# Split first weight units, two constants DMAs, and a new order of the first products in a one-core hybrid decoder block

## Chip, core and metric

One NeuronCore of a Trainium2 chip runs the whole program in one launch. The metric is device time in microseconds (us). Engines are called by the names of the profile: PE is TensorE's matmul side and PEld its weight loads, DVE is VectorE, ACT is ScalarE, POOL is GpSimd, and SP is SyncE, which here only issues DMAs.

## What is computed

The block takes x (512 tokens by 2048 channels, float32) through one decoder layer. Cut to what matters:

```python
h = rms_norm(x, norm1_g)
proj = h @ w_in                       # 2048 x 3840: 30 tiles of 128 columns
out_a = dilated_mixture(aq, ak, av)   # 8 heads x 64
out_b = conformer_conv(bu, bg, ...)   # GLU, depthwise conv of 31 taps, LayerNorm, swish
out_c = band_attention(cq, ck, cv, 127, sinks)
x = x + concat(out_a, out_b, out_c) @ w_out
h2 = rms_norm(x, norm2_g)
x = x + (silu(h2 @ w_gate) * (h2 @ w_up)) @ w_down
```

The change touches only the start of `h @ w_in`: the four column tiles bu0, bg0, bu1, bg1 that are computed first, while x and the first weights are still on their way from HBM.

## The kernel before

Everything is held transposed: a tile of x is 128 channels by 512 tokens, so x comes in 16 tiles `xs[k]`, k = 0 to 15 (256 KB each, loaded by `load_first`). A float32 product is made of three fp32r products. A weight block is split into `wh` (its fp32r rounding, a CAST on ACT, line 242) and `wl` (the rest, a subtraction on DVE, line 229). The scaled input is split likewise by `scaled`: `hh` on ACT (line 368), `hl` on DVE (line 369). `mm3` then issues wh with hh, wh with hl and wl with hh (lines 271, 272, 273) into one PSUM bank.

The first stage, called the head here, fills four PSUM banks at once (`g4`, tile name `in`): for each k, four column tiles times three products, twelve matmuls of 128x512. All 16 values of k make 192 matmuls. Weights of the head come as units: unit 0 and unit 1 are the two 512-column halves of the first 1024-column block (k = 0 and k = 1, 256 KB each), and every later unit of the head is a whole block of 512 KB that serves two values of k. In the profile these tiles are called `w`, their halves `wh` and `wl`.

Three things set the order of the work. `pump` issues the weight DMAs on SP's queue in the order of `units`, as far as raw buffers (`RAW_PLAIN`, used in rotation) are free; calls of `load_first` lie between them on the same queue. `split_up_to` issues the CAST and the subtraction of a unit, up to two units ahead of its use; ACT and DVE work strictly down the list in which Python issued their instructions. `WARM` dummy matmuls on a tile `idle`, filled by a DVE memset, are issued on PE ahead of the head. While the head runs, ACT and DVE also square x and add the squares up (`add_square`, lines 374, 377, 378) for the RMS norm.

The per-channel constants (norm gains, convolution weights, gains and sinks) come in one array `cst` of 188 columns by one DMA, which is the first instruction on ACT's queue (line 277). Columns 0 to 15 are the gains of the first norm, used by `scaled`; the others are used after the head.

Waits are made by semaphores. The DMAs get their completion semaphores from a set of eight in turn, in the order of the DMAs. A DMA that takes over a semaphore waits in its issuing engine's instruction list until the DMA that held it before has landed.

Of the kernel before, what the change touches and what calls it, by code (L numbers as in the profile page):

```python
# [9 lines left out]
F32 = mybir.dt.float32  # L10
F32R = mybir.dt.float32r
BF16 = mybir.dt.bfloat16
# [4 lines left out]
P = 128  # L17
T = 512
NT = T // P
D = 2048  # L20
KT = D // P
HD = 64
# [5 lines left out]
N_IN = 30  # L28
# [21 lines left out]
RAW_PLAIN = "22b sb 21a 22a 11 sa 12".split()  # L50
RAW_BUFS = 8
RAW_EARLY = 5
SPLIT_BUFS = 3
X_AHEAD = 8
SPLIT_AHEAD = 2
WARM = 10

# [5 lines left out]
TH = T // 2  # L65
# [17 lines left out]
C_G1, C_G2, C_CW, C_CB, C_LG, C_LB, C_QK, C_SINK, C_ALL = 0, 16, 32, 156, 160, 164, 168, 172, 188  # L83
# [34 lines left out]
def kernel(ctx: ExitStack, tc: tile.TileContext, xT, wi, wo, wgu, wd, cst_in, outT):  # L118
    nc = tc.nc
    cp = ctx.enter_context(tc.tile_pool(name="consts", bufs=1))  # L120
# [17 lines left out]
    def slot(name, dt=F32, cols=T):  # L138
        return sp.tile([P, cols], dt, name=name, tag="s")

    def bank(name, cols=T):
        return psum["banks"].tile([P, cols], F32, name=name, tag="b")


    units = [wi[0][:, :T], wi[0][:, T:]] + [wi[u] for u in range(1, 2 * N_IN)]
    units += [wo[2 * n + half] for half in range(2) for n in OUT_ORDER[half]]


    entries, works = [], []
# [4 lines left out]
    def take(buf, key, n=1024):  # L154
        assert buf not in held
        held[buf] = key
        raws[key] = (wp.tile([P, 1024], F32, name=f"w{key}", tag=f"raw{buf}", bufs=1), n)
        return raws[key][0]

    def drop(key):  # L160
        for buf in [b for b, k in held.items() if k == key]:
            held.pop(buf)
        return raws.pop(key)

    for u, unit in enumerate(units):
        entries.append((RAW_PLAIN[u % len(RAW_PLAIN)], u, [unit]))
        works.append((u, True, nc.vector))

    def group(name, m, n, blocks):
# [41 lines left out]
    splits = {}  # L211
    at = {"entry": 0, "split": 0, "use": 0}

    def pump(limit):
        while at["entry"] < len(entries) and len(raws) < limit and entries[at["entry"]][0] not in held:
            buf, key, parts = entries[at["entry"]]
            t, o = take(buf, key, sum(p.shape[-1] for p in parts)), 0
            for part in parts:
                nc.sync.dma_start(t[:, o:o + part.shape[-1]], part)
                o += part.shape[-1]  # L220
            at["entry"] += 1
# [4 lines left out]
    def lows_now():  # L226
        while lows:
            fn, *args = lows.pop(0)
            fn(*args)  # L229
        if late_lows:  # L230
            pump(RAW_EARLY if at["use"] <= 20 else RAW_BUFS)

    def split_up_to(i):
        while at["split"] <= min(i, len(works) - 1):
            key, last, eng = works[at["split"]]
            t, n = drop(key) if last else raws[key]
            u = at["split"]
            hi = wp.tile([P, 1024], F32R, name=f"wh{u}", tag="hi", bufs=SPLIT_BUFS)
            lo = wp.tile([P, 1024], F32R, name=f"wl{u}", tag="lo", bufs=SPLIT_BUFS)
            if eng or "high" not in psum:  # L240
                eng = eng or nc.vector
                nc.scalar.copy(hi[:, :n], t[:, :n])  # L242
                lows.append((eng.tensor_sub, lo[:, :n], t[:, :n], hi[:, :n].bitcast(F32)))
                if not late_lows:
                    lows_now()
            else:
                near = psum["high"].tile([P, 1024], F32R, name=f"wn{u}", tag="h")
                nc.scalar.copy(near[:, :n], t[:, :n])
                nc.scalar.copy(hi[:, :n], t[:, :n])  # L249
                lows.append((nc.vector.tensor_sub, lo[:, :n], t[:, :n], near[:, :n].bitcast(F32)))  # L250
                if not late_lows:
                    lows_now()
            splits[u] = (hi, lo)
            at["split"] += 1
# [5 lines left out]
    def next_unit():  # L260
        sums_now()
        u = at["use"]
        at["use"] += 1
        lows_now()
        split_up_to(u + SPLIT_AHEAD)
        if not lows:
            pump(RAW_EARLY if u < 20 else RAW_BUFS)
        return splits.pop(u)

    def mm3(out, wh, wl, xh, xl, start, stop):  # L270
        nc.tensor.matmul(out, wh, xh, start=start, stop=False)  # L271
        nc.tensor.matmul(out, wh, xl, start=False, stop=False)  # L272
        nc.tensor.matmul(out, wl, xh, start=False, stop=stop)  # L273


    cst = cp.tile([P, C_ALL], F32, name="cst")
    nc.scalar.dma_start(cst, cst_in)
    xs = []

    def load_first(k):  # L280
        x = slot(f"x{k}")
        nc.sync.dma_start(x, xT[k])
        xs.append(x)

    for k in range(X_AHEAD):
        load_first(k)
        u = k if k < 2 else k // 2 + 1
        if u < RAW_EARLY and (k < 2 or k % 2 == 0):
            pump(u + 1)


    idle = slot("idle", BF16)
    nc.vector.memset(idle, 1.0)
    b = bank("idle")
    for i in range(WARM):
        nc.tensor.matmul(b, idle[:, :P], idle, start=True, stop=True)
    b = idle = None

    nhalf = cp.tile([P, 8], F32, name="nhalf")
# [4 lines left out]
    make_identity(nc, ident)  # L304
    ones = cp.tile([P, 1], F32, name="ones")
    nc.vector.memset(ones, 1.0)
    bones = cp.tile([P, 2], F32, name="bones")
    nc.vector.memset(bones, 0.0)
    nc.vector.memset(bones[0:HD, 0:1], 1.0)
    nc.vector.memset(bones[HD:P, 1:2], 1.0)  # L310

    def col(i):
        return cst[:, i:i + 1]
# [52 lines left out]
    def scaled(x, g, tag, k):  # L366
        hi, lo = slot(f"{tag}h{k}", F32R), slot(f"{tag}l{k}", F32R)
        nc.scalar.activation(hi, x, AF.Copy, scale=g)
        nc.vector.scalar_tensor_tensor(lo, x, g, hi.bitcast(F32), op0=ALU.mult, op1=ALU.subtract)
        return hi, lo  # L370

    def add_square(acc, x, k, tag):
        if k == 0:
            nc.scalar.activation(acc, x, AF.Square)
        else:
            sq = slot(f"{tag}{k}")
            nc.scalar.activation(sq, x, AF.Square)
            nc.vector.tensor_add(acc, acc, sq)
# [9 lines left out]

    g4 = [bank(f"in{j}") for j in range(HEAD4)]
    h_hl = {}  # L390
    for k in range(2):
        h_hl[k] = scaled(xs[k], col(C_G1 + k), "h", k)
        split_up_to(k)
    pump(RAW_EARLY)
    add_square(ssum, xs[0], 0, "sq")
    for k in range(KT):
        if k < 2 or k % 2 == 0:
            wh, wl = next_unit()
            o = 0
        if k + X_AHEAD < KT:  # L400
            load_first(k + X_AHEAD)
        if k + 2 < KT:
            h_hl[k + 2] = scaled(xs[k + 2], col(C_G1 + k + 2), "h", k + 2)
        if k + 1 < KT:
            add_square(ssum, xs[k + 1], k + 1, "sq")
        hi, lo = h_hl.pop(k)
        h_hi.append(hi)
        h_lo.append(lo)
        for j in range(HEAD4):
            mm3(g4[j], wh[:, o:o + P], wl[:, o:o + P], hi, lo, k == 0, k == KT - 1)  # L410
            o += P
    xs = None
    c64 = cp.tile([P, NT], F32, name="c64")
# [7 lines left out]
    def project(name):  # L421
        b = bank(name)
        for half in range(2):
            wh, wl = next_unit()
            for kk in range(8):
                k = 8 * half + kk
                s = slice(kk * P, (kk + 1) * P)
                mm3(b, wh[:, s], wl[:, s], h_hi[k], h_lo[k], k == 0, k == KT - 1)
                if kk == 3:
                    lows_now()  # L430
                if kk % 2 == 1:
                    ticks.tick()
        return b
# [348 lines left out]
    g4 = None  # L782
# [15 lines left out]
    part = {}  # L798
    for name in PROJ[HEAD4:]:
        kind, what, j = name[0], name[1], name[2:]  # L800
# [3 lines left out]
        b = project(name)  # L804
# [19 lines left out]
    b = box = boxes = shared = None  # L824
# [81 lines left out]
    for half in range(2):  # L906
        for i, n in enumerate(OUT_ORDER[half]):
            if half == 1 and i == 2:
                ticks.drain()
                b = None  # L910
                open_banks(banks=4, high=2)
            b = bank(f"o{half}_{n}")
            wh, wl = next_unit()
            for kk in range(8):
                k = 8 * half + kk
# [262 lines left out]
    for g in range(2 * NP + len(DOWN)):  # L1178
        t = g - 2 * NP
# [4 lines left out]
        else:  # L1184
            n, first, end = DOWN[t]
            blk = Down(t)
        for i, q in enumerate(ORDER):
            sums_now()
            run(evacs)
            w = next_unit()  # L1190
# [109 lines left out]
```

## Time and profile before

| What | Value |
|---|---|
| Median of 3 runs (1899.9 to 1900.35) | 1900.18 us |
| The profiled execution's own time | 1899.99 us |
| Its span, first to last instruction | 1898.2 us |
| Lies around the span | 1.79 us |
| Mean granted TensorE clock | 0.999 |
| Busy: PE, DVE, ACT, POOL | 1887.0, 1467.6, 1330.7, 996.1 us |

Times in rows of the profile are counted from the start of the span. In a timeline row the first number is the start, the second the duration, then come engine, line, operation, output and inputs; a bracket tells how long the engine was idle before and what released it. SPq and ACTq rows are the issuing of DMAs on the queues of SP and ACT, not the transfers. In rows of DMA issues the last number is the time from the start of the issue to the landing of the data.

### The profile page before, as it was taken

The numbers are of one execution on the slowest core, as the hardware profiler recorded it, in microseconds if no ns is written. First come the engines' busy times: TensorE is split into PE (matmuls) and PEld (weight loads), VectorE is DVE, ScalarE is ACT, GpSimd is POOL, SyncE is SP. The second block draws the span as 40 slices with busy tenths as digits, with TensorE's granted clock in tenths as the row PEclk, the third lists the DMA queues.
The fourth block names the chain that finished last, engine by engine and source line by source line (L and its number), as shares of the span: only waits on it lengthen the run. The fifth ranks groups of instructions, "written<-read, shape, count | busy, mean of one in ns | idle before, by whom it ended". The sixth has DMA issues, their size and how long they took to land.

```text
span 1898.2 us, 29669 instructions
## 1 busy us (share of the span) xinstructions
PE 1887.0 (99%) x10342; PEld 1636.9 (86%) x10342; DVE 1467.6 (77%) x2561; ACT 1330.7 (70%) x1855; POOL 996.1 (52%) x643
## 2 busy tenths in 40 slices
PE   9999999999999999999999999999999999999999
PEld 7888888878888888888888888888888888888888
DVE  6789978998679777777777777777787877677776
ACT  6356645453357888888888888888887777766775
POOL 0111011000002878788787878787767656565775
PEclk9999999999999999999999999999999999999999
DMA  7342242433342444445454554445456887777985
GB/s 268 88 129 79 77 130 83 112 106 117 123 140 98 141 153 162 144 149 174 141 165 139 165 168 150 155 136 187 140 167 238 269 268 263 266 249 231 315 263 202
DMA packets 136310, 320.29 MB, mean 169 GB/s; under 512 B 15584, under 2 KB 31072, under 8 KB 136160
## 3 DMA queue, kind: packets, MB, share of 16 engines
q1 hardware_dynamic: 136016, 318.31, 52.0%
q8 instruction: 81, 1.33, 0.3%
q14 instruction: 69, 0.57, 0.1%
q10 hardware_dynamic: 144, 0.10, 0.0%
HBM read 254.11 MB, written 55.84 MB: 163 GB/s over the span
## 4 chain that ended last, share of the span: by engine, by line
PE 94%; DVE 4%; ACT 1%; issue 0%; DMA 0%; SPq 0%; DVEq 0%; ACTq 0%
PE out L989 68%; PE o L271 2%; PE o L272 2%; PE o L273 2%; PE cq L271 2%; PE cq L273 2%; PE cq L272 2%; PE ak L271 1%; PE ak L273 1%; PE ak L272 1%; PE in L272 1%; PE av L271 1%; PE av L272 1%; PE in L273 1%; PE av L273 1%; PE in L271 1%
## 5 line engine op out<-in xcount | busy, mean ns | idle before, releaser
L989 PE MATMUL out<-h,wh 128*128 128x512 f32 x2464 | 588.8, 391 | 1.0 <-DVE h L899 0.8
L989 PEld LDWEIGHTS out<-h,wh 128*128 128x128 f32 x2464 | 452.7, 188 | 89.3 <-DVE h L899 1.3
L989 PEld LDWEIGHTS out<-h,wl 128*128 128x128 f32 x2464 | 316.0, 191 | 12.0
L989 PE MATMUL out<-h,wl 128*128 128x256 f32 x2464 | 319.9, 283 | 0.0
L989 PE MATMUL out<-a,wh 128*128 128x512 f32 x1232 | 296.2, 391 | 0.0
L989 PEld LDWEIGHTS out<-a,wh 128*128 128x128 f32 x1232 | 225.7, 188 | 43.6 <-ACT wh L249 0.4
L242 ACT CAST wh<-w 128x1024 fp32r<-128x1024 f32 (+1 forms) x93 | 96.8, 1041 | 113.0 <-PE o L272 48.8
L989 PEld LDWEIGHTS out<-a,wl 128*128 128x128 f32 x1232 | 159.4, 191 | 6.9
L989 PE MATMUL out<-a,wl 128*128 128x256 f32 x1232 | 161.5, 283 | 0.0
L229 DVE TENSOR_TENSOR wl<-w,wh 128x1024 fp32r<-128x1024 f32 (+1 forms) x93 | 112.3, 1209 | 45.1 <-ACT wh L242 44.7
L458 DVE SCALAR_TENSOR_TENSOR y<-bu,cst,y 128x511 f32<-128x511 f32 (+14 forms) x120 | 89.5, 746 | 0.2
L1001 DVE TENSOR_TENSOR y<-y,out 128x256 f32<-128x256 f32 x93 | 39.1, 420 | 46.1 <-PE out L989 44.4
L271 PE MATMUL cq<-hh,wh 128*128 128x512 f32 x128 | 51.2, 400 | 0.5 <-DVE mix_c L743 0.5
L271 PE MATMUL o<-mh_c,wh 128*128 128x512 f32 x128 | 51.6, 403 | 0.0
L273 PE MATMUL o<-mh_c,wl 128*128 128x512 f32 x128 | 50.5, 394 | 0.0
L272 PE MATMUL o<-ml_c,wh 128*128 128x512 f32 x128 | 50.4, 394 | 0.0
L273 PE MATMUL cq<-hh,wl 128*128 128x512 f32 x128 | 50.0, 391 | 0.0
L272 PE MATMUL cq<-hl,wh 128*128 128x512 f32 x128 | 50.0, 390 | 0.0
L1002 DVE TENSOR_TENSOR y<-y,out 128x256 f32<-128x256 f32 x101 | 42.5, 421 | 3.5
L386 POOL TENSOR_TENSOR lvr<-lvv,nhalf 128x4 f32<-128x4 f32 x1 | 1.9, 1931 | 76.7 <-DVE lvv L385 76.7
L184 POOL TENSOR_TENSOR w('s', 'g1')_5687<-w('21', 'g1')_5533,w('22', 'g1')_5531 128x1024 f32<-128x1024 f32 x1 | 2.5, 2457 | 71.0 <-DVE wl L229 71.0
L849 DVE TENSOR_TENSOR xr<-xr,o 128x512 f32<-128x512 f32 x32 | 21.8, 682 | 13.9 <-PE o L273 13.8
(3135 smaller groups left out, 4869.1 us busy)
## 6 DMA issues: line engine op xcount, KB each, us to landing
a<-od SPq DMA_DIRECT2D x175, 256.0 KB, 5.2
od<-a SPq DMA_DIRECT2D x147, 256.0 KB, 4.6
w<-in_wi SPq DMA_DIRECT2D x59, 512.0 KB, 3.6
w<-in_wo SPq DMA_DIRECT2D x32, 512.0 KB, 3.6
yd<-y SPq DMA_DIRECT2D x68, 128.0 KB, 4.8
y<-yd SPq DMA_DIRECT2D x34, 256.0 KB, 5.1
x<-in_xT SPq DMA_DIRECT2D x16, 256.0 KB, 7.5
xr<-in_xT SPq DMA_DIRECT2D x16, 256.0 KB, 3.8
```

The costliest lines, as they stand in the source:

```text
L184: eng.tensor_add(out[:, :n], raws[key[a]][0][:, :n], raws[key[b]][0][:, :n])
L229: fn(*args)
L242: nc.scalar.copy(hi[:, :n], t[:, :n])
L271: nc.tensor.matmul(out, wh, xh, start=start, stop=False)
L272: nc.tensor.matmul(out, wh, xl, start=False, stop=False)
L273: nc.tensor.matmul(out, wl, xh, start=False, stop=stop)
L386: nc.gpsimd.tensor_tensor(r, v, nhalf[:, :NT], op=ALU.pow)
L458: nc.vector.scalar_tensor_tensor(yconv[j][:, i:], hconv[j][:, :T - i], c, yconv[j][:, i:], op0=ALU.mult, op1=ALU.add)
L849: nc.vector.tensor_add(t, t, b)
L989: nc.tensor.matmul(out, lhs[:, s], rhs, start=begin, stop=x is xs[-1] and low == flip[0], skip_group_check=True)
L1001: sign(out, out if first is None else first, main)
L1002: sign(out, out, rest)
```

## The change

Unit 0 is cut into two units of 256 columns (128 KB each), so that the units are numbered one higher from there on: what was unit 1 (k = 1) is unit 2 and what was unit 2 (k = 2 and 3) is unit 3. The CAST of the new unit 0 is done on DVE. The constants come in two DMAs on ACT's queue: columns 0 to 15 as its first instruction, columns 16 to 187 after the memset of `ones`, still ahead of the first `scaled`. The twelve products of k = 0 are issued in another order, two at a time: hh with both upper halves, then hh with wl of unit 0, hl with both, hh with wl of unit 1. `scaled` of k + 2 is issued ahead of the split of the next unit. The dummy matmuls go from ten to eight, and their 512 columns are 128 columns read four times, so that the memset is of 128 columns. The tile `bones`, which nothing read, goes with its three memsets.

```diff
-WARM = 10
+WARM = 8
...
-    units = [wi[0][:, :T], wi[0][:, T:]] + [wi[u] for u in range(1, 2 * N_IN)]
+    units = [wi[0][:, :TH], wi[0][:, TH:T], wi[0][:, T:]] + [wi[u] for u in range(1, 2 * N_IN)]
...
-        entries.append((RAW_PLAIN[u % len(RAW_PLAIN)], u, [unit]))
+        entries.append((RAW_PLAIN[(u - 1) % len(RAW_PLAIN)], u, [unit]))
...
-                nc.scalar.copy(hi[:, :n], t[:, :n])
+                (nc.vector.tensor_copy if u == 0 else nc.scalar.copy)(hi[:, :n], t[:, :n])
...
-    nc.scalar.dma_start(cst, cst_in)
+    nc.scalar.dma_start(cst[:, :C_G2], cst_in[:, :C_G2])
...
     for k in range(X_AHEAD):
         load_first(k)
-        u = k if k < 2 else k // 2 + 1
-        if u < RAW_EARLY and (k < 2 or k % 2 == 0):
-            pump(u + 1)
+        if k < 2 or k % 2 == 0:
+            pump(min(k + 2 if k < 2 else k // 2 + 3, RAW_EARLY))
-    idle = slot("idle", BF16)
+    idle = slot("idle", BF16, P)
     nc.vector.memset(idle, 1.0)
     b = bank("idle")
     for i in range(WARM):
-        nc.tensor.matmul(b, idle[:, :P], idle, start=True, stop=True)
+        nc.tensor.matmul(b, idle, idle[:, None, :].to_broadcast([P, NT, P]), start=True, stop=True)
...
     nc.vector.memset(ones, 1.0)
-    bones = cp.tile([P, 2], F32, name="bones")
-    nc.vector.memset(bones, 0.0)
-    nc.vector.memset(bones[0:HD, 0:1], 1.0)
-    nc.vector.memset(bones[HD:P, 1:2], 1.0)
+    nc.scalar.dma_start(cst[:, C_G2:], cst_in[:, C_G2:])
...
-    for k in range(2):
-        h_hl[k] = scaled(xs[k], col(C_G1 + k), "h", k)
-        split_up_to(k)
+    split_up_to(0)
+    h_hl[0] = scaled(xs[0], col(C_G1), "h", 0)
+    split_up_to(1)
+    h_hl[1] = scaled(xs[1], col(C_G1 + 1), "h", 1)
+    split_up_to(2)
     pump(RAW_EARLY)
     add_square(ssum, xs[0], 0, "sq")
     for k in range(KT):
-        if k < 2 or k % 2 == 0:
+        if k + 2 < KT:
+            h_hl[k + 2] = scaled(xs[k + 2], col(C_G1 + k + 2), "h", k + 2)
+        if k == 0:
+            at["use"] = 2
+            first = [splits.pop(u) for u in range(2)]
+        elif k == 1 or k % 2 == 0:
             wh, wl = next_unit()
             o = 0
         if k + X_AHEAD < KT:
             load_first(k + X_AHEAD)
-        if k + 2 < KT:
-            h_hl[k + 2] = scaled(xs[k + 2], col(C_G1 + k + 2), "h", k + 2)
         if k + 1 < KT:
             add_square(ssum, xs[k + 1], k + 1, "sq")
         hi, lo = h_hl.pop(k)
         h_hi.append(hi)
         h_lo.append(lo)
+        if k == 0:
+            for part, u in ((0, 0), (0, 1), (2, 0), (1, 0), (1, 1), (2, 1)):
+                for j in range(2):
+                    w = first[u][part == 2][:, j * P:(j + 1) * P]
+                    nc.tensor.matmul(g4[2 * u + j], w, (hi, lo, hi)[part], start=part == 0, stop=False)
+            first = w = None
+            continue
         for j in range(HEAD4):
-            mm3(g4[j], wh[:, o:o + P], wl[:, o:o + P], hi, lo, k == 0, k == KT - 1)
+            mm3(g4[j], wh[:, o:o + P], wl[:, o:o + P], hi, lo, False, k == KT - 1)
             o += P
```

## Prediction

> **What bounds the kernel now.** I read the page first, then who PE waited for, then the first 13 us engine by engine, since all the edits lie there. From the page:
>
> ```profile
> span 1898.2 us, 29669 instructions
> PE 1887.0 (99%) x10342; PEld 1636.9 (86%) x10342; DVE 1467.6 (77%) x2561; ACT 1330.7 (70%) x1855; POOL 996.1 (52%) x643
> ```
>
> PE is idle for 11.2 us in all. Whatever delays its first products delays the end, unless a later wait shrinks. PE's waits over the whole span, by releaser (total us, times, longest):
>
> ```profile
> PE a2o L730 <- DVE a2pl L716: 2.5, 1, 2.5
> PE idle L296 <- DVE bones L308: 1.5, 1, 1.5
> PE o L271 <- DVE xr L849: 0.9, 1, 0.9
> PE out L989 <- DVE h L899: 0.8, 1, 0.8
> PE a3o L730 <- DVE a3pl L716: 0.5, 1, 0.5
> PE cq L271 <- DVE mix_c L743: 0.5, 1, 0.5
> PE in L272 <- DVE hl L369: 0.2, 1, 0.2
> PE out L989 <- ACT wh L249: 0.2, 1, 0.2
> ```
>
> After the head all releasers are DVE or ACT work that itself comes out of earlier products of PE; no DMA is among them. So these waits move along with the head and absorb nothing: a microsecond lost or won in the head should show whole at the end. The question is when the head gets going. SP's queue, and the chain that ended last within the first 13 us:
>
> ```profile
> 2.59 0.43 SPq L282 DMA_DIRECT2D x<-in_xT  x1
> 3.06 0.43 SPq L219 DMA_DIRECT2D w<-in_wi  x1
> 3.54 1.05 SPq L282 DMA_DIRECT2D x<-in_xT  x2
> 7.84 0.33 SPq L282 DMA_DIRECT2D x<-in_xT  x1
> ```
>
> ```profile
> 3.06 6.10 DMA w<-in_wi
> 9.19 1.05 ACT wh L242
> ```
>
> The rows at 2.59, 3.06 and 3.54 are x2, unit 2 (512 KB) and x3 with x4. Unit 2 lands at 3.06 + 6.10 = 9.16, and from there ACT's CAST leads on to the products of k = 2. When the two tiles of x landed (last number: us from issue):
>
> ```profile
> x<-in_xT SPq DMA_DIRECT2D x1, 256.0 KB, 5.2
> ```
>
> ```profile
> x<-in_xT SPq DMA_DIRECT2D x1, 256.0 KB, 6.3
> ```
>
> x2: 2.59 + 5.2 = 7.8; x3: 3.54 + 6.3 = 9.8. The row at 7.84 is x7, the fourteenth DMA. It takes over the semaphore that x2, the sixth, held, and it starts 0.05 us after x2 landed: a DMA whose semaphore is still held waits in its queue, and what stands behind it waits too. Now ACT, DVE and PE in the head:
>
> ```profile
> 0.73 0.41 ACTq L277 DMA_DIRECT2D cst<-in_cst  x1
> 1.17 1.28 ACT L302 ACT_TABLE_LOAD   x1 [1.17 <-PEq L1291]
> 4.07 0.72 ACT L368 ACTIVATE hh<-x,cst 128x512 fp32r<-128x512 f32 x1 [1.40 <-DMA cst<-in_cst]
> 5.07 0.62 ACT L242 CAST wh<-w 128x512 fp32r<-128x512 f32 x1 [0.28 <-DMA w<-in_wi]
> 7.73 0.63 ACT L374 ACTIVATE ssum<-x 128x512 f32<-128x512 f32 x1
> ```
>
> ```profile
> 0.91 0.48 DVE L293 MEMSET idle<- 128x512 bf16 x1 [0.91 <-PEq L1291]
> 1.61 0.06 DVE L310 MEMSET bones<- 64x1 f32 x1
> 4.82 0.75 DVE L369 SCALAR_TENSOR_TENSOR hl<-x,cst,hh 128x512 fp32r<-128x512 f32 x1 [3.16 <-ACT hh L368]
> 5.72 0.69 DVE L229 TENSOR_TENSOR wl<-w,wh 128x512 fp32r<-128x512 f32 x1
> 10.27 1.23 DVE L229 TENSOR_TENSOR wl<-w,wh 128x1024 fp32r<-128x1024 f32 x1 [1.72 <-ACT wh L242]
> ```
>
> ```profile
> 1.45 4.14 PE L296 MATMUL idle<-idle 128*128 128x512 bf16 x10 [1.45 <-DVE bones L308]
> 5.74 0.50 PE L271 MATMUL in<-hh,wh 128*128 128x512 f32 x1
> 8.89 0.39 PE L271 MATMUL in<-hh,wh 128*128 128x512 f32 x1
> 11.61 0.39 PE L271 MATMUL in<-hh,wh 128*128 128x512 f32 x1
> 12.55 0.39 PE L273 MATMUL in<-hh,wl 128*128 128x512 f32 x1
> ```
>
> The rows at 5.74, 8.89 and 11.61 are the first products of k = 0, 1 and 2. Twelve products take 11.61 - 8.89 = 2.72 us, 0.227 each. The row at 12.55 is the third product of k = 2; from it on PE runs without a pause in the head. I use it as the mark: its shift is the shift of the end.
>
> **The wait that the change adds.** The instruction lists of the two built programs show an edit that the diff does not say. In the changed kernel ACT's list begins so:
>
> ```
> DMACopy cst<-in_cst 128x16
> LoadActFuncSet
> Activation early<-nhalf 128x1        [waits DVE]
> DMACopy cst<-in_cst 128x172          [waits DMA semaphore 7]
> Activation hh0<-x0,cst 128x512       [waits DMA semaphores 1 and 0]
> ```
>
> The eight semaphores go 0 to the first constants, then on SP's queue x0, w0, w1, x1, w2, x2, and 7 to w3. The second constants DMA takes over number 7 from w3, the 512 KB block for k = 2 and 3. ACT must therefore wait for the landing of w3 before it may issue, and behind that DMA stands all of ACT's work on the head: hh0, wh1, hh1, wh2 and so on. Behind ACT wait DVE (hl0 needs hh0) and PE (its first product needs hh0).
>
> When w3 lands: ahead of it and with it SP's queue carries 256 + 128 + 128 + 256 + 256 + 256 + 512 = 1792 KB. Before, up to the same block, it was 256 + 256 + 256 + 256 + 256 + 512, also 1792 KB. It is issued one step of 0.47 us later (3.06 - 2.59), which is covered: by 4 us only 165 x 4 = 660 KB had moved.
>
> ```profile
> 0.00:4.00 4.00, 2.55 (x7) 0.90 (x8) 0.64 (x6) 1.49 (x2) 1.51 (x8) 1.00 0.49 165
> ```
>
> (That is the window's row: length, busy us of PE, PEld, DVE, ACT, POOL, granted clock, DMA share, GB/s.) The first constants shrink from 94 KB, with this row, to 8 KB:
>
> ```profile
> cst<-in_cst ACTq DMA_DIRECT2D x1, 94.0 KB, 3.3
> ```
> From 4 us to 9.16 us at least 1792 + 94 - 660 = 1226 KB moved, 238 KB a us, so 86 KB less is at most 0.4 us earlier. Against that the two quarter units have 256 rows of 1 KB in place of 128 of 2 KB, whose price no row shows; I bound it by the same 0.4 us later. I take 9.16.
>
> Then the sum, each duration from the rows above. ACT: issue at 9.18 and 0.41 long (the row at 0.73), hh0 from 9.62 to 10.34. PE's first product follows 0.05 us later, as it followed the CAST before (5.07 + 0.62 to 5.74): 10.39. ACT goes on: wh1, 256 columns, estimated 0.41 (0.62 at 512, 1.05 at 1024), to 10.75; hh1 to 11.47; wh2 0.62 to 12.09; ssum 0.63 to 12.72; hh2 to 13.44; the square, like ssum, to some 14.06; hh3 to 14.78; wh3 1.05 to 15.83. DVE's wl3 takes 1.23 more, to 17.08, and the mark follows at 17.11.
>
> **At which pace PE comes out of the wait.** At full pace the 24 products of k = 0 and 1 take 24 x 0.227 = 5.4 us from 10.39, to 15.83. So the mark is set by wl3: 17.11 - 12.55 = 4.56 us late. But PE does not always run at that pace. Its weight loads for the dummies:
>
> ```profile
> 1.86 0.15 PEld L296 LDWEIGHTS <-idle 128*128 128x128 bf16 x1 [0.28 <-issue]
> 4.84 0.15 PEld L296 LDWEIGHTS <-idle 128*128 128x128 bf16 x1 [0.28 <-issue]
> ```
>
> Seven steps in 2.98 us: 0.426 each for 512 columns, though the granted clock of that window stands at 1.00. So the first 4.14 us of work, after nothing, ran at little over half pace, and the products from 5.74 on at full pace. In the changed kernel the dummies begin at 1.45 or sooner (shorter memset) and eight take 8 x 0.426 = 3.4 us, over by 5; then PE has nothing until 10.39, over 5 us. Whether it comes out slow no row shows, as PE never waits so long in this trace. The nearest row is the start itself: slow after nothing, for 4.14 us. I take that: 4.14 / 0.426 = 9.7 products in the slow stretch, the other 14.3 at 0.227 = 3.25 us, so k = 2 starts at 10.39 + 4.14 + 3.25 = 17.78. By then wl3 is there, and the third product starts at 17.78 + 0.45 = 18.23: 5.68 us late.
>
> [...]
>
> **The other edits.** The DVE cast and subtraction of unit 0 (each at most 0.69) are done long before hh0; DVE waited 3.16 us there already. Three bones memsets of 0.06 lay in the same gap. Two dummies fewer, the broadcast read and the shorter memset end ahead of the first product by 5 us: nothing, unless they are why PE is slow, which the range holds. The new product order is worth nothing here, since hl0 and wl1 (DVE: 11.1 and 11.5) are made before PE reaches them. SP's queue does not wait for ACT until buffers must come free: w7 goes where w0 was, long free, and the 512 KB blocks w4 to w7 cover PE through k = 11. The second constants land some 3.3 us after 9.2 and are used after the head. Without the new wait, hh3 before wh3 would itself cost a little (below).
>
> **Rivals.** First, PE comes out of the wait at full pace: +4.56, so 1904.7. For it speaks only that the dummies ran before; against it the start. Chance 0.22.
>
> Second, not slower: ACT passes the waiting DMA, if issuing is a list of its own (the rows are marked ACTq, apart from ACT). Then hh0 runs at 4 us and PE's 24 products are over by 11.7. hh3 now stands before wh3 and needs x3, landed at 9.8: hh3 to 10.6, wh3 to 11.6, wl3 to 12.9, the mark at 12.93, +0.4 against before; x3 up to 0.4 earlier makes it even. So 1900.2 to 1900.6, no change. It decides if hh0 starts before about 5 us. Against it: the table load began at 1.17, just when the first issue had ended (0.73 + 0.41), and SP's queue stands still at such a wait. Chance 0.09. [...]
>
> Third, w3 lands over 0.7 us earlier and PE keeps its pace: under +3.8, about 1903.5. Chance 0.03.
>
> **The numbers.** The forecast, the slow restart, has 0.66. On the profiled execution's own 1899.99 (0.19 under the median) +5.68 gives 1905.67, on the median of 1900.18 it gives 1905.9, which I predict. Low end: full pace and w3 earlier by the 0.4 and a little more, +3.8: 1904.0. High end: a slow stretch half as long again, 6.2 us (14.6 products, then 9.4 at 0.227, the mark at 19.2, +6.6) and w3 0.4 late: 1907.3. About what a measurement of this kernel can tell from no change is 0.2%, 3.8 us. Slower by more: the forecast and nearly all of the first rival, 0.87; within: 0.12, the other rivals; faster: 0.01, since no case here gives so much.
>
> **What would show it.** In the profile after: ACT's second cst issue near 9.2 and hh0 near 9.6, with a wait of some 7 us ahead of them; PE's first real product near 10.4; weight loads of the first eight to fifteen products about 0.43 apart, then 0.227; the third product of k = 2 near 18.2, and later waits of PE as before. hh0 near 4 us would prove the forecast wrong; first products 0.23 apart would prove the first rival right.

## The result and the profile after

The changed kernel takes 1905.65 us (median of 7 runs, 1904.96 to 1906.55), the kernel before 1899.59 us (7 runs, 1898.14 to 1900.35): 6.06 us more. The ratio is 1.0034, with a 95% interval of 1.0025 to 1.0043. The profiled execution took 1905.44 us with a span of 1903.7 us, 5.5 us above the span before.

The page says nearly nothing. PE's busy time grew by only 0.4 us (slow products added to it, two dummies fewer took from it), so 5.1 us of the loss is idle time of PE:

```profile
span 1903.7 us, 29671 instructions
PE 1887.4 (99%) x10340; PEld 1638.3 (86%) x10340; DVE 1468.3 (77%) x2560; ACT 1330.1 (70%) x1855; POOL 995.8 (52%) x643
```

PE's waits name it, in one row. Those further down the list are those of before:

```profile
PE in L417 <- ACT hh L365: 6.0, 1, 6.0
PE a2o L741 <- DVE a2pl L727: 2.7, 2, 2.5
PE idle L296 <- DVE ones L306: 1.1, 1, 1.1
```

The timeline of ACT in the head (start, duration, and in the bracket the idle time before):

```profile
2.46 0.20 ACT L302 ACTIVATE early<-nhalf 128x1 f32<-128x1 f32 x1
9.14 0.33 ACTq L307 DMA_DIRECT2D cst<-in_cst  x1
9.59 0.72 ACT L365 ACTIVATE hh<-x,cst 128x512 fp32r<-128x512 f32 x1 [6.92 <-DMA x<-in_xT]
10.21 0.39 ACT L243 CAST wh<-w 128x256 fp32r<-128x256 f32 x1
```

ACT issues the second constants DMA at 9.14, and only then comes hh0. Here the bracket misleads: it puts the 6.92 us down to a DMA of x. x0 had landed at 3.4 (issued at 0.73, 2.7 us to landing) and the first constants at 3.6:

```profile
x<-in_xT SPq DMA_DIRECT2D x1, 256.0 KB, 2.7
cst<-in_cst ACTq DMA_DIRECT2D x1, 8.0 KB, 2.9
```

The issue of w3 on SP, and the times to landing of w3 and x3:

```profile
3.54 0.43 SPq L219 DMA_DIRECT2D w<-in_wi  x1
```

```profile
w<-in_wi SPq DMA_DIRECT2D x1, 512.0 KB, 5.6
x<-in_xT SPq DMA_DIRECT2D x1, 256.0 KB, 5.8
```

w3 landed at 3.54 + 5.6, some 9.1 us, just when the ACTq row begins. x3, issued at 4.01, landed only at 9.8, when hh0 was already running. The bracket names x3 all the same: x3 had taken over the semaphore of the first constants, on which hh0 also waits, and the parts of x3 that came in from 9.06 to 9.80 counted it up. PE after the wait:

```profile
1.05 3.30 PE L296 MATMUL idle<-idle 128*128 128x512 bf16 x8 [1.05 <-DVE ones L306]
10.36 2.08 PE L417 MATMUL in<-hh,wh 128*128 128x512 f32 x4 [6.00 <-ACT hh L365]
14.97 0.39 PE L272 MATMUL in<-hh,wh 128*128 128x512 f32 x1
17.72 0.39 PE L272 MATMUL in<-hh,wh 128*128 128x512 f32 x1
18.17 0.39 PE L274 MATMUL in<-hh,wl 128*128 128x512 f32 x1
```

The rows at 14.97 and 17.72 are the first products of k = 1 and 2. The twelve products of k = 0 take 14.97 - 10.36 = 4.61 us, those of k = 1 take 2.75 us. The mark, the third product of k = 2, stands at 18.17 against 12.55. The windows show why k = 0 is slow (the third number from the end is the granted clock):

```profile
5.00:10.00 5.00, 0.00 (x0) 0.00 (x0) 0.00 (x0) 0.41 (x1) 0.00 (x0) 0.73 1.00 355
10.00:14.00 4.00, 3.64 (x9) 2.88 (x10) 3.44 (x6) 4.00 (x8) 0.00 (x0) 0.50 1.05 399
14.00:16.00 2.00, 2.00 (x10) 1.65 (x9) 1.67 (x3) 1.83 (x3) 0.00 (x0) 0.96 1.01 398
```

The clock fell to half while PE had nothing to do (a mean of 0.73 from 5 to 10 us is full clock for 46% of it, so the fall came near 7.3, some 3 us after the dummies), and it stayed at 0.50 until about 14 us.

### The profile page after: what moved, and what is told of

It is laid out like the page before. It is cut to its first block, busy times and chain, and to the rows that moved or that the text cites. A ratio compares the mean times of both kernels' runs of the same rounds, so it can differ in the third digit from the quotient of the medians.

```text
span 1903.7 us, 29671 instructions
## 1 busy us (share of the span) xinstructions
PE 1887.4 (99%) x10340; PEld 1638.3 (86%) x10340; DVE 1468.3 (77%) x2560; ACT 1330.1 (70%) x1855; POOL 995.8 (52%) x643
## 4 chain that ended last, share of the span: by engine, by line
PE 94%; DVE 4%; ACT 1%; issue 0%; DMA 0%; SPq 0%; DVEq 0%; ACTq 0%
PE out L1000 67%; PE o L272 2%; PE o L273 2%; PE o L274 2%; PE cq L272 2%; PE cq L274 2%; PE cq L273 2%; PE ak L272 1%; PE ak L274 1%; PE ak L273 1%; PE in L273 1%; PE in L274 1%; PE in L272 1%; PE av L272 1%; PE av L273 1%; PE av L274 1%
## 5 line engine op out<-in xcount | busy, mean ns | idle before, releaser
L229 DVE TENSOR_TENSOR wl<-w,wh 128x1024 fp32r<-128x1024 f32 (+2 forms) x94 | 112.4, 1198 | 45.7 <-ACT wh L243 45.4
```

## The experiments

Two theories are on trial. The main one: ACT stands at the second constants DMA until the semaphore's holder lands, then PE starts at a fallen clock. Its rivals: hh0 waits for the landing of x3, as the bracket seems to say; or another part of the change costs the time.

**The second DMA, later.** It is issued at the end of the head; nothing else is touched.

```diff
-    nc.scalar.dma_start(cst[:, C_G2:], cst_in[:, C_G2:])
...
             load_first(k + X_AHEAD)
+        if k == KT - 1:
+            nc.scalar.dma_start(cst[:, C_G2:], cst_in[:, C_G2:])
```

> The changed kernel, with one edit: the second constants DMA is issued at the end of the head (k = 15) and not before the first scaled, so that ACT meets no held semaphore. All else of the change stays. Theory (ACT stands at the second constants DMA until w3 lands): hh0 starts when x0 and the 8 KB of constants are there, near 3.7 us and not at 9.59; first product of PE near 4.4; w3 still lands near 9.1 and x3 near 9.6; hh3 stands ahead of wh3, so wh3 ends near 11.3, wl3 near 12.5, and the third product of k = 2 starts near 12.6, as before (12.55). Time within 1 us of the kernel before, some 5.5 to 6 us under the changed kernel. Rival (hh0 waits for the landing of x3 at 9.55, as the row of the profile names it, or the head is bound by the transfers in their new order): hh0 stays near 9.6 and the time near 1905.5.

1900.33 us against 1899.44 us before; ratio 1.0005, interval 0.9996 to 1.0014. ACT and PE in its head:

```profile
3.63 0.72 ACT L364 ACTIVATE hh<-x,cst 128x512 fp32r<-128x512 f32 x1 [0.96 <-DMA cst<-in_cst]
10.03 0.72 ACT L364 ACTIVATE hh<-x,cst 128x512 fp32r<-128x512 f32 x1 [0.35 <-DMA x<-in_xT]
10.66 1.03 ACT L243 CAST wh<-w 128x1024 fp32r<-128x1024 f32 x1
13.00 0.50 PE L274 MATMUL in<-hh,wl 128*128 128x512 f32 x1 [0.53 <-DVE wl L229]
```

hh0 starts at 3.63, although x3 lands at 10.0 (the row at 10.03 is hh3, which waits for it). So x3 does not hold hh0, and the bracket of the changed kernel misleads. (The 9.55 of the expectation is the moment at which the profile ends that bracket's wait; x3 landed at 9.8 there.) All but about half a microsecond of the loss is gone. The rest is the new order, as the next run shows: hh3 stands ahead of wh3 in ACT's list and waits for x3, and wh3, wl3 and the mark follow.

**That, and the split of unit 3 ahead of scaled of k = 3.**

```diff
     for k in range(KT):
+        if k == 1:
+            split_up_to(3)
         if k + 2 < KT:
             h_hl[k + 2] = scaled(...)
```

> As the kernel with the late second constants DMA, and the split of unit 3 (w3) is issued ahead of scaled of k = 3, so that wh3 does not stand behind hh3, which needs x3. Theory: with the wait gone, the landing of w3 near 9.1 sets the head: wh3 to 10.2, wl3 to 11.4, third product of k = 2 near 11.5, 1.0 us earlier than before; time 1.0 us under the kernel before (half a per mille, at the edge of what the runs tell), 6.5 to 7 us under the changed one. Rival (the order of hh3 and wh3 does not matter, PE is not there yet): the third product stays near 12.6, as in the run with the late DMA alone.

1898.91 us against 1899.44 us; ratio 0.9997, interval 0.9988 to 1.0006: the runs don't tell it from no change. In its profile the mark came at 11.74, 0.8 us ahead of before and 1.3 us ahead of the run with the late DMA alone, and the span was 1897.4 us. The order matters, by about what the theory asked; the landing of w3 at 9.1 does not quite set the mark, since wh3 began at 9.39, behind a square of x on ACT.

**Dummies through the wait.** `WARM = 8` becomes `WARM = 33`; the wait stays.

> The changed kernel with 33 dummy matmuls in place of 8, so that PE is busy up to the first product near 10.4. The wait of ACT stays. Theory (PE falls back to the slow pace while it has nothing to do, and the 4 us after the wait run slow): products start near 10.4 at 0.227 apart from the first one on; wl3 then sets the third product of k = 2, near 16.4 (18.17 in the changed kernel); time 1.5 to 2 us under the changed kernel. Rival (the slow first products come from something else, for example from waits for hl0 and wl1, or from the product order): the third product stays near 18.2.

1903.46 us; ratio to before 1.0022, interval 1.0013 to 1.0032. The granted clock is 1.00 in every window from 0 to 20 us, and the first products run at full pace:

```profile
1.06 9.34 PE L296 MATMUL idle<-idle 128*128 128x512 bf16 x33 [1.06 <-DVE ones L306]
10.49 1.19 PE L417 MATMUL in<-hh,wh 128*128 128x512 f32 x4
13.34 0.39 PE L272 MATMUL in<-hh,wh 128*128 128x512 f32 x1
16.52 0.40 PE L274 MATMUL in<-hh,wl 128*128 128x512 f32 x1
```

Twelve products of k = 0 take 13.34 - 10.49 = 2.85 us, and the mark comes at 16.52, 1.65 us ahead of the changed kernel. So of the 5.62 us at the mark, 1.65 us are the fallen clock and 3.97 us the wait itself. Here w3 landed 0.13 us later than in the changed kernel; counted from the first product to the mark, 6.03 us against 7.81 us, the fallen clock costs 1.78 us, which leaves 3.84 us for the wait.

**One dummy.** `WARM = 1`.

> The changed kernel with one dummy matmul in place of eight. Theory (PE falls back to the slow pace in the wait whatever ran before it): first product near 10.4, ten or so products 0.43 apart, third product of k = 2 near 18.2 as with eight, span near 1903.7. Rival (the eight dummies carry part of the pace over the wait): more slow products, third product of k = 2 at 19 or later.

One run: 1905.91 us, span 1904.1 us. w3 landed half a microsecond later in this execution, so PE's first product came at 10.89 and the mark at 18.67. From the one to the other it takes 7.78 us, against 18.17 - 10.36 = 7.81 us with eight dummies. As far as one run shows, the eight carry nothing over the wait.

**The two DMAs alone, in the kernel before.**

```diff
-    nc.scalar.dma_start(cst, cst_in)
+    nc.scalar.dma_start(cst[:, :C_G2], cst_in[:, :C_G2])
...
     nc.vector.memset(bones[HD:P, 1:2], 1.0)
+    nc.scalar.dma_start(cst[:, C_G2:], cst_in[:, C_G2:])
```

> The kernel before, with one part of the change alone: the constants in two DMAs, the second at the same place of ACT's list (ahead of the first scaled). Units, order of products and ten dummies as before. In the built program the second DMA takes over the semaphore of x3 here, not of w3. Theory: ACT stands until x3 lands near 9.8, hh0 starts near 10.3, PE near 11.7, after an idle of 6 us at the slow pace, and the third product of k = 2 starts near 19.5: 7 us later than before, time near 1906.5. Rival (the split of the units or the new order costs the time, the second DMA little): hh0 near 4 us, time as before.

1907.11 us; ratio 1.0041, interval 1.0027 to 1.0054. This part alone costs more than the whole change, because the semaphore is x3's here, which landed at 9.64 and so later than w3 in the changed kernel (9.1), and because PE's first product waits for one more step:

```profile
9.67 0.34 ACTq L311 DMA_DIRECT2D cst<-in_cst  x1
10.11 0.72 ACT L369 ACTIVATE hh<-x,cst 128x512 fp32r<-128x512 f32 x1 [7.44 <-DMA x<-in_xT]
```

PE starts at 11.39, since wh0 is a CAST of 512 columns on ACT in this kernel; ten products are 0.43 apart, and the mark comes at 19.59, 7.04 us late (7 were expected).

**One constants DMA again** in the changed kernel:

> The changed kernel with the constants in one DMA again, as before; the split units, the new orders and eight dummies stay. Theory (all of the loss came from the wait of the second DMA; what is left is bound by the landing of x3, since hh3 stands ahead of wh3): hh0 near 4.1, when 94 KB of constants have landed; third product of k = 2 near 13.0, as with the late second DMA; time within 0.5 us of that run (1900.3), so the small first DMA buys nothing at the mark. Rival (an earlier hh0 is worth its 0.4 us): the third product 0.4 us later than with the late DMA, near 13.4.

1900.2 us; ratio 1.0005, interval 0.9996 to 1.0015. hh0 starts at 4.12, half a microsecond later than with 8 KB, and the mark came at 13.33, which is the rival's number. But it is not the rival's cause: hh3 waited for x3 here until 10.35 (10.03 above), and from hh3 to the mark it takes 2.98 us here and 2.97 us there. The landing of x3 sets the mark, and the early hh0 buys nothing. Whether the 86 KB more in front delayed x3, or it was this execution, is taken up with the second fallen clock.

**Both DMAs at the head of ACT's list**, one behind the other:

> The changed kernel with the second constants DMA issued right behind the first on ACT, where it takes a fresh semaphore. Theory: no wait on ACT; its issue takes 0.4 us more ahead of the table load, which nobody waits for; hh0 near 3.8, third product of k = 2 near 13.0, time near 1900.3. Rival (it is not the held semaphore but any second DMA on ACT's list ahead of hh0 that costs the time): hh0 near 9.6 and time near 1905.5.

1900.61 us; ratio 1.0006, interval 0.9997 to 1.0016; hh0 at 3.65, the mark at 12.89. So a second DMA ahead of hh0, on a semaphore that nobody holds, did not hold hh0 up here (3.63 with the late DMA, 9.59 in the changed kernel). In the changed kernel it stands in the same list, only later in the rotation.

**A second fallen clock.** Two spans did not fit the mark. From the mark to the end, before takes 1898.2 - 12.55 = 1885.65 us, and the changed kernel, the late DMA, the reordered one, 33 dummies, one dummy and the two DMAs alone take 1885.4 to 1885.7 us. With one constants DMA it was 1897.5 - 13.33 = 1884.2 us, with the pair 1899.5 - 12.89 = 1886.6 us. The windows found the place, behind the 2.5 us in which PE waits for a2pl. Before from 418 to 422 us, with the granted clock in the third number from the end:

```profile
418.00:420.00 2.00, 2.00 (x7) 1.57 (x6) 1.93 (x6) 0.58 (x1) 0.00 (x0) 0.54 0.00 0
420.00:422.00 2.00, 2.00 (x9) 1.61 (x8) 2.00 (x4) 1.64 (x2) 0.00 (x0) 0.61 0.33 70
```

The window from 410 to 440 us of before, of the kernel with one constants DMA, and of the pair:

```profile
410.00:440.00 30.00, 27.32 (x126) 22.43 (x125) 24.66 (x52) 11.90 (x20) 1.64 (x1) 0.94 0.56 165
```

```profile
410.00:440.00 30.00, 27.35 (x133) 22.53 (x133) 25.98 (x59) 13.05 (x21) 1.64 (x1) 1.00 0.58 167
```

```profile
410.00:440.00 30.00, 27.49 (x122) 22.74 (x121) 23.89 (x51) 11.71 (x18) 1.64 (x1) 0.89 0.51 148
```

A mean of 0.94 over 30 us is some 3.6 us at half clock; 0.89 is some 6.6 us, and 1.00 none. (The means have two digits. Cut into windows of 0.1 us, before is at half clock from 418.16 to 421.58, 3.42 us, and the pair from 416.78 to 423.61, 6.83 us.) Before and the six kernels that agree with it all have 0.94. So behind the same wait stands one stretch of half clock, two or none, and the spans that don't fit the mark are explained.

The mean granted clocks of all executions say the same. Of the 67 executions of the kernel before that were measured beside the experiments, 16 have a mean granted clock of 1.000 and 51 have 0.999 or 0.998. In each of the three groups that were measured together, the executions at 1.000 are all faster than the others (1897.91 to 1898.66 us against 1899.04 to 1900.26 us in the first), and the medians lie 1.5, 1.8 and 1.1 us apart. A median over all executions mixes the two kinds, so a small difference shows better within one kind. Median of each kernel less that of before, at equal mean clock (four executions at 0.998 are left out):

| Kernel | At 0.999 (executions) | At 1.000 (executions) |
|---|---|---|
| Late second DMA | +0.5 us (10) | +0.6 us (1) |
| That, reordered | -0.6 us (8) | -0.2 us (3) |
| 33 dummies | +3.7 us (7) | +4.2 us (2) |
| One constants DMA | +1.2 us (5) | +1.3 us (5) |
| Both DMAs at the head | +0.6 us (6) | +0.6 us (1) |

The last two were measured together, and one DMA of 94 KB is 0.7 us slower than two. So the 86 KB more in front most likely do cost; in the profiles x3 landed at 10.3 with one DMA and at 9.9 with two, which fits but is one execution each.

Two kernels fill that wait with matmuls of zeros into the bank that is being summed (they add nothing), the reordered kernel and the kernel before:

```diff
+    zb = cp.tile([P, 4], BF16, name="zb")
+    nc.gpsimd.memset(zb, 0.0)
...
+                        if name == "a2" and h == 0 and t == 1 and o == 0:
+                            for _ in range(13):
+                                nc.tensor.matmul(out, zb[:, :1].to_broadcast([P, P]), zb[:, :1].to_broadcast([P, n]),
+                                                 start=False, stop=False, skip_group_check=True)
                         nc.tensor.matmul(out, v, pl[t][:, o:o + n], start=False, stop=last, skip_group_check=True)
```

> The kernel with the late second constants DMA and the earlier split of unit 3, with 13 matmuls of zeros (128x384, they add nothing to the sums) put into the 2.5 us in which PE waits for a2pl in the attention stage near 414 us. Theory (the same fall-back of the clock as in the changed head: the wait at 414 us lets the granted clock drop to 0.5 for some 3 us in most executions, and executions without the drop are 1.5 us shorter): granted clock 1.00 from 414 to 430, third product of k = 2 near 11.7 as without the zeros, span near 1896.0 to 1896.5; median near 1897.6, 2 us under the kernel before and 8 under the changed one. Rival (the drop comes with the mix of work there and not with the wait, or the zeros delay the waiting products): clock still near 0.5 somewhere from 414 to 430, span 1897.4 or more.

> The kernel before, with the same 13 matmuls of zeros in the wait near 414 us, and without the unread tile bones, whose room they need. Theory: granted clock 1.00 from 414 to 430, head as before (third product of k = 2 near 12.5), span near 1896.7; median 1.0 to 1.5 us under the kernel before. Rival: no change in clock and time.

Both have 1.00 from 410 to 440 us in their profiles, and all 22 executions of the two have a mean granted clock of 1.000, against 3 of the 21 of before beside them. The filled reordered kernel:

```profile
410.00:440.00 30.00, 29.47 (x147) 23.71 (x146) 25.98 (x59) 13.13 (x21) 1.64 (x1) 1.00 0.53 162
```

The reordered and filled kernel takes 1898.13 us against 1899.71 us, ratio 0.9991, interval 0.9982 to 0.9999: the one version whose interval lies under 1, and only just. The filled kernel before takes 1898.15 us, ratio 0.9993, interval 0.9984 to 1.0002. From the mark to the end both take 1884.0 us (1896.3 - 12.29 and 1896.2 - 12.20), 1.6 us less than before. The reordered head itself gave nothing here: w2 landed at 7.73 (7.17 without the zeros) and wh3 began at 9.94 (9.39), so that its mark came at 12.29, not near 11.7, while unit 2 of the filled kernel before landed at 8.8 (9.2 without). The medians of the two are equal too. So the gain comes from the zeros, and the reordering is worth between 0 and 0.8 us.

## Why the prediction was right, step by step

*The whole head shift passes to the end.* Right: 5.62 us at the mark, 5.5 us at the span, 6.06 us between the medians, where 5.68 us was predicted. That the time itself came within 0.3 us of the 1905.9 us predicted is luck in part: that number stood on 1900.18 us for before, which came out at 1899.59 us in seven runs. Six kernels with marks from 11.74 to 19.59 keep 1885.5 us from mark to end within 0.2 us, as before does; all seven profiles hold one fall of the clock behind the wait for a2pl.

*ACT stands at the second DMA until w3 lands.* Right in place and time: the issue at 9.14 (9.18 predicted), hh0 at 9.59 (9.62), the first product at 10.36 (10.39). That the landing was met so closely is luck in part: with the same DMAs w3 landed at 9.25 in the run with 33 dummies and at 9.65 in that with one. The run with the late DMA shows that it is this wait, and the run of the two DMAs alone that it follows the holder of the semaphore. The ACTq row comes at the landing (9.14, w3 at 9.12), and ACT does nothing from 2.66 until then.

*PE comes out of the wait slowly.* Right, and shown by the runs with 33 dummies and with one. The length was near, with some luck. The 4.14 us were the time of all ten dummies, the last of which ran at full clock: in the trace of before the clock rises at 5.15, 3.70 us after the first dummy. In the changed kernel it rises at 14.17, 3.81 us after the first product; with one dummy that took 3.73 us, with the two DMAs alone 4.59 us. The clock fell at 7.34, 3.0 us after the last dummy. What was wrong is that no row of before shows whether PE comes out of a wait slow: the window from 418 to 422 us shows it behind a wait of 2.54 us (0.54 and 0.61), and would have raised the chance of this case.

*The price of the rival with a full clock* was too high: +4.56 us, where 33 dummies measured +3.97 us. The failed term is the sum over ACT's list. It added full durations, but the next ACT instruction starts about 0.1 us before the one ahead of it ends (hh0 at 9.59 for 0.72 us, wh1 at 10.21). Over the eight instructions up to wh3 that is 0.8 us. So wl3 was ready in time (near 16.35), and PE set the mark itself: 26 products from 10.49 at 0.23 are 6.0 us. In the forecast the error was hidden, since there the slow products set the mark and not wl3.

*The rival in which ACT passes the DMA* fell. Its price, +0.4 us for hh3 ahead of wh3, was measured without the wait: 13.00 - 12.55 = 0.45 us.

*The other edits at nothing.* Nearly right. With the wait gone, three versions of the changed kernel lie 0.6 to 1.0 us above before, with 1.0 inside each interval of the ratio; at equal mean clock they lie 0.5 to 1.3 us above it. The +0.4 us that the prediction gave to hh3 ahead of wh3 covers most of the 0.5 to 0.6 us of the late DMA and of the pair.

## What to carry to other kernels

Splitting a DMA took one more place in the rotation of the semaphores here, and the DMA that took a held semaphore kept ACT idle from 2.66 to 9.14, with every later instruction of ACT behind it: look in the built program at what each DMA on a computing engine waits for, and issue it either while fresh semaphores remain (hh0 at 3.65 here) or after the urgent work (3.63). The wait of PE of 6.0 us cost 1.65 us at the mark beyond the wait itself, because the clock fell; read the granted clock of the windows behind each long wait of PE, and fill the wait if the clock drops there (1.6 us less from mark to end here). Where a bracket names a releaser that had long landed, or had not landed yet, look for a wait of the instruction ahead in the list.

## What the runs showed of the hardware

A wait of PE of 2.5 us was followed by a fall of the clock to half, and the fall came after PE was back at work: before, the wait ended at 416.72 and the clock fell at 418.16.

```profile
416.72 0.44 PE L730 MATMUL a2o<-a2pl,av 128*128 128x384 f32 x1 [2.54 <-DVE a2pl L716]
```

The same wait led to 3.4 us of half clock in seven profiles (3.42 us in before), to 6.83 us in that of the pair and to none in that with one constants DMA.

The traces of before and after show more: in both, the changes of the clock lie whole multiples of 3.413 us apart. Before they lie at 5.15, 418.16 and 421.58, which is 121 of these steps and one; after at 3.93, 7.34, 14.17, 423.77 and 427.18, which is one, two, 120 and one. The windows of the two DMAs alone agree: a fall near 9.1, a rise near 15.96 and a fall near 425.56 are two steps and 120 apart. In the step at whose end the clock fell, PE had been idle in the wait for a2pl for 1.59 us (the two DMAs alone), 1.97 us (before), 2.00 us (after) and 2.48 us (33 dummies). With one constants DMA the spacing of the products goes from 0.46 to 0.24 us near 6.75; if the clock rose there, 120 such steps end near 416.35 and cut the wait (415.15 to 417.65) into some 1.2 us and 1.3 us, and the clock stayed. The wait is 2.5 us long in each of these five profiles, so its length does not tell them apart, while its place on the steps does; that this is the cause is not shown. Nor is it shown why the fall of the pair lasted two steps; its wait ended at 417.18, 0.40 us after the fall at 416.78, while in the other four that fell the wait was over before the fall.

The granted clock of the windows missed a slow stretch. With one dummy the column reads 1.00 from 0 to 14 us:

```profile
10.00:14.00 4.00, 3.11 (x7) 2.51 (x8) 2.91 (x5) 3.88 (x8) 0.00 (x0) 1.00 1.04 402
```

Seven products in 3.1 us, 0.44 each, is the slow pace all the same. In the traces of before and after the first entry of the clock is its rise to full (at 5.15 and 3.93), and ahead of it the column reads 1.00 although the dummies are 0.426 us apart, so at the start of these kernels the spacing of the products has to be read instead.
